# Hybrid decoder step on one Trainium2 core: hops of the stream merges moved within a step, up-projections ahead of turned probabilities, and two cache halves in other attention steps

## The chip, the cores and the metric

The kernel runs on one core of a Trainium2 chip. A core has four engines that compute, each with an instruction stream of its own, worked off in order: TensorE (PE, matrix products into PSUM), VectorE (DVE), ScalarE (ACT) and GpSimd (POOL). DMA queues move data between HBM and on-chip memory (SBUF); here SyncE, ScalarE and GpSimd issue them. The metric is the device time of one execution in microseconds (us), lower is better.

## The reference

One step of a two-layer decoder trunk serves a prompt of 1024 new tokens and 8 decode sequences of one token each. Layer 0 mixes with an mLSTM, layer 1 with multi-head latent attention; each is followed by a dense SwiGLU block. The change touches only the attention of layer 1, where both groups attend:

```python
def mla_attend_prompt(q_lat, q_rope, c_kv, k_r):   # per block of queries
    s = einsum('bqhc,bkc->bhqk', ql, c_kv) + einsum('bqhr,bkr->bhqk', qr, k_r)
    p = softmax(where(causal, s * MLA_SCALE, -inf))
    return einsum('bhqk,bkc->bqhc', p, c_kv)

def mla_attend_sample(q_lat, q_rope, c_new, kr_new, cache_latent, cache_k_rope, page_table, layer_idx):
    # per decode sequence: 8192 cached rows, read through a page table, and one new row
    c_all = concatenate([cache_latent[layer_idx, pages].reshape(past, 256), cn])
    kr_all = concatenate([cache_k_rope[layer_idx, pages].reshape(past, 64), krn])
    p = softmax((einsum('qhc,kc->hqk', ql, c_all) + einsum('qhr,kr->hqk', qr, kr_all)) * MLA_SCALE)
    return einsum('hqk,kc->qhc', p, c_all)
```

The outputs are the hidden states of both groups, the mLSTM states and the new latent and rotary rows.

## The kernel before

**Prompt attention** is cut into 32 blocks, one for each head and each group of 256 queries; a block of group G (0 to 3) attends to 2G + 2 tiles of 128 keys. A block's work is: two *scores* (`scores(0)` and `scores(1)`, one for each 128 queries, L1768 to L1775, with the row maximum on VectorE, L1776, and the exponential on ScalarE, L1785), *scale* (reciprocal on VectorE, L1793, and a pass over the probabilities on ScalarE, L1795), *turn* (128x128 transposes of the probabilities on TensorE, L1811, in groups of up to four, each emptied from PSUM into a high and a low part: ScalarE copies, L359 and L360, and GpSimd subtracts, L361; for the group on the diagonal ScalarE, L348, and VectorE, `wl`, L349), and *values* (L1833, three products for each key tile) with a copy out on ScalarE (L1836). Scores have four PSUM banks (`sc`), turns and values two (`mm`), the decode part two (`ss`). The keys and values of each head are *up-projected* from the latent rows (`make_k`, `make_v`, L365 to L367), emptied the same way.

A loop of 29 *steps* (`slot` 1 to 29 in the code) works on two blocks at a time: step s turns block s and does its values, and does scores and scale of block s + 1. Even heads take their groups in the order 0, 1, 2, 3, odd heads in the order 3, 2, 1, 0, so steps 3, 4, 11, 12, 19, 20 and 27 have the longest blocks and steps 7, 8, 15, 16, 23 and 24 the shortest. Steps 4, 12, 20 (group 3) and 2, 10, 18, 26 (group 2) hold a `make_k`; 5 to 7, 13 to 15, 21 to 23, and 8, 16 and 24 a `make_v`; steps 1, 3, 9, 11, 17, 19, 25 and 27 to 29 hold none.

**Decode attention** runs beside it as 32 *halves* (`Half`), each of 2048 cached rows: two halves make a unit, and two units make one decode sequence. For a half, GpSimd gathers the latent rows (`nat`, 2 MB in two indirect DMAs, four buffers) and the rotary rows (`nrp`, 0.5 MB, two buffers); VectorE transposes them in five pieces (`turn` in class `Sample`, tiles `tt`, L134, four buffers); TensorE multiplies them with the queries (`scores` in `Sample`, L143, 48 and 32 products). The code speaks of `first`, `second`, `third` and `fourth` of a half: `first` multiplies pieces 1, 4 and 0 and turns pieces 2 and 3 and piece 4 of the next half, `second` turns piece 0 of the next half and multiplies pieces 3 and 2, `third` turns piece 1 of the next half, `fourth` begins the softmax of the unit (`soft`) if the half is the second of a unit. In the step after that the probabilities are transposed and copied into place (`probs`, `pz`, L158, twelve copies on ScalarE and four on VectorE), and the *sums* (L173, 64 products) multiply them with both `nat` tiles of the unit, which frees these for the gathers of the halves four and five further on.

After the second unit of a sequence a *meeting* (`meet`) merges the parts of the 16 key streams: ten *hops* f0 to f9, alternately on VectorE ("V") and TensorE ("P"), in the order V P V P V V P V P V. The TensorE hops are L231, L239, L249 and L257. `hop(e)` issues the next one if it is for engine e, so a step's calls of `hop` say where each stands. Before, a step has the calls: V in `first`, P at the start of `second`, V at the end of `third`, P right before values, V in `fourth`; a meeting takes two steps.

TensorE's order is the order of the code. The other engines' orders are set by a scheduler from its own estimates, so they are to be read from the built program. SyncE only issues loads here.

## Time and profile before

| | us |
|---|---|
| median of 3 runs (2778.24 to 2785.95) | 2785.31 |
| profiled execution, its own time | 2779.62 |
| its span in the profile | 2777.1 |
| mean granted TensorE clock | 0.968 |
| step 1 of the loop starts about | 1424 |
| step 29 ends about | 1903 |

The attention loop is 479 of the 2777 us. Steps are told apart by the copy that ends each one's values (L1836): step 4 runs from about 1490 to 1506, step 5 to 1522, step 7 from 1533 to 1546, step 8 to 1559, step 12 from 1617 to 1640, step 19 from 1731 to 1752, step 21 from 1770 to 1783, step 22 to 1795, step 23 to 1809, step 26 from 1847 to 1870.

A row of a time line gives start, duration, engine, line, operation, what is written and read, and in brackets the idle time of the engine before it and what ended it. A row of a list of waits gives who waited for whom, the total, how many times, and the longest.

### The profile page before, as it was taken

What the parts mean: (1) busy time and instruction counts of PE and PEld (TensorE: products, weight loads), DVE (VectorE), ACT (ScalarE), POOL (GpSimd) and SP (SyncE); (2) the same over time, 40 slices, a digit from 0 to 9 for tenths busy, and PEclk for the clock granted to TensorE, in tenths of its full rate; (3) what the DMA queues carried; (4) which work ended last, traced back from release to release, by engine and by line L of the source; (5) the groups of instructions that cost most, each with busy time, mean ns of one, the idle gap of its engine ahead of it and who ended that gap; (6) DMA issues with size and microseconds to landing.
All of it is one profiled execution on the core that took longest, in us unless ns stands there. A gap on an engine that the chain in (4) does not pass through costs nothing.

```text
span 2777.1 us, 51994 instructions
## 1 busy us (share of the span) xinstructions
PE 2584.3 (93%) x20719; PEld 2442.9 (88%) x20719; DVE 1476.9 (53%) x3141; ACT 1194.5 (43%) x2715; POOL 868.4 (31%) x831
## 2 busy tenths in 40 slices
PE   8999989889999999999868887979988999999998
PEld 8998877889999999998757676767888999999997
DVE  4346678853344343455456667666574443434455
ACT  4212334434444444444246465645344444444442
POOL 1001002243333333323234454432323333333342
PEclk9999989999999999999879999989999999999999
DMA  5133556336655655453575657573533656555552
GB/s 183 38 76 95 129 144 155 106 86 129 119 115 116 123 116 117 86 188 119 160 266 179 220 196 261 200 256 97 192 100 86 125 117 124 116 116 117 117 140 100
DMA packets 350424, 383.67 MB, mean 138 GB/s; under 512 B 24441, under 2 KB 303358, under 8 KB 341862
## 3 DMA queue, kind: packets, MB, share of 16 engines
q0 software_dynamic: 38736, 174.68, 26.5%
q1 hardware_dynamic: 284502, 189.12, 23.2%
q10 hardware_dynamic: 26944, 16.56, 2.5%
q8 instruction: 162, 2.65, 0.4%
q14 instruction: 80, 0.66, 0.1%
HBM read 254.58 MB, written 125.70 MB: 137 GB/s over the span
## 4 chain that ended last, share of the span: by engine, by line
PE 66%; DVE 11%; DMA 11%; issue 5%; ACT 4%; POOL 3%; SPq 0%; ACTq 0%; POOLq 0%; DVEq 0%
PE sc L365 9%; PE sc L367 9%; PE sc L366 9%; PE ss L365 5%; PE ss L366 5%; PE mm L365 5%; PE ss L367 5%; PE mm L366 5%; PE mm L367 5%; DMA Gb<-G_d 2%; DMA nat<-in_cache_latent_dram,idx 2%; PE ss L143 2%; DVE wl L349 1%; PE mm L1833 1%; DVE tt L134 1%
## 5 line engine op out<-in xcount | busy, mean ns | idle before, releaser
L365 PE MATMUL ss<-ah,dh 128*128 128x344 f32 x864 | 277.5, 321 | 7.1 <-ACT st L1309 6.6
L1309 ACT COPY st<-ss 128x344 f32<-128x344 f32 x432 | 189.9, 441 | 215.4 <-PE ss L367 183.4
L366 PE MATMUL ss<-al,dh 128*128 128x344 f32 x864 | 277.6, 321 | 1.9 <-POOL al L349 1.9
L367 PE MATMUL ss<-ah,dl 128*128 128x344 f32 x864 | 276.9, 320 | 0.0
L348 ACT ACTIVATE wh<-wr 128x512 fp32r<-128x512 f32 (+2 forms) x161 | 130.6, 812 | 236.2 <-PE mm L366 127.2
L1311 POOL DMA_DIRECT2D x_d<-st x144 | 124.8, 867 | 244.1 <-ACT st L1309 240.2
L134 DVE STREAM_TRANSPOSE tt<-nat 128x1024 f32<-128x1024 f32 x128 | 156.8, 1232 | 52.3 <-PE ss L143 29.3
L365 PEld LDWEIGHTS ss<-ah,dh 128*128 128x128 f32 x864 | 163.0, 189 | 8.3 <-ACT st L1309 7.3
L366 PEld LDWEIGHTS ss<-al,dh 128*128 128x128 f32 x864 | 163.4, 189 | 2.3 <-POOL al L349 2.3
L349 POOL TENSOR_TENSOR al<-u,ah 128x512 fp32r<-128x512 f32 (+1 forms) x84 | 118.4, 1410 | 148.2 <-ACT ah L348 148.1
L367 PEld LDWEIGHTS ss<-ah,dl 128*128 128x128 f32 x864 | 163.1, 189 | 0.0
L349 DVE TENSOR_TENSOR wl<-S,wl 128x512 fp32r<-128x512 f32 x89 | 77.8, 874 | 156.9 <-ACT wl L348 125.8
L349 DVE TENSOR_TENSOR wl<-wr,wh 128x1024 fp32r<-128x1024 f32 (+2 forms) x92 | 106.0, 1153 | 51.2 <-ACT wh L348 43.4
L349 DVE TENSOR_TENSOR wh<-S,wh 128x512 fp32r<-128x512 f32 x91 | 68.6, 754 | 119.1 <-ACT wh L348 91.3
L1275 DVE TENSOR_TENSOR u<-u,sc 128x260 f32<-128x260 f32 (+1 forms) x168 | 70.8, 421 | 114.2 <-PE sc L367 113.0
L143 PE MATMUL ss<-tt,qbd 128*32 128x128 f32 x2560 | 98.4, 292 | 28.4 <-DVE tt L134 17.8
L1241 POOL TENSOR_TENSOR S<-S,wr 128x512 f32<-128x512 f32 x45 | 62.9, 1397 | 175.4 <-DVE wh L349 87.9
L1234 POOL TENSOR_TENSOR S<-wr 128x512 f32<-128x512 f32 x45 | 61.5, 1367 | 164.5 <-DMA wr<-in_ffn_w_gate_up_dram 162.0
L143 PEld LDWEIGHTS ss<-tt,qbd 128*32 128x32 f32 x2560 | 74.7, 117 | 41.6 <-issue 24.9
L365 PE MATMUL mm<-zh,wh 128*128 128x344 f32 x320 | 104.7, 327 | 7.0 <-DVE ot L693 6.9
L349 DVE TENSOR_TENSOR dl<-dr,dh 128x256 fp32r<-128x256 f32 x144 | 69.1, 480 | 73.0 <-ACT dh L348 73.0
L366 PE MATMUL mm<-zl,wh 128*128 128x344 f32 x320 | 103.8, 324 | 0.0
(928 smaller groups left out, 9226.7 us busy)
## 6 DMA issues: line engine op xcount, KB each, us to landing
x_d<-st POOLq DMA_DIRECT2D x144, 516.0 KB
wr<-in_ffn_w_gate_up_dram SPq DMA_DIRECT2D x98, 512.0 KB
dr<-in_ffn_w_down_dram SPq DMA_DIRECT2D x144, 128.0 KB
wr<-in_mlstm_w_in_dram SPq DMA_DIRECT2D x24, 512.0 KB
wr<-in_mlstm_w_out_dram SPq DMA_DIRECT2D x16, 512.0 KB
q<-qn_d SPq DMA_DIRECT2D x32, 256.0 KB
wr<-in_mla_w_o_dram SPq DMA_DIRECT2D x15, 512.0 KB
qn_d<-qx SPq DMA_DIRECT2D x16, 344.0 KB
```

The costliest lines, as they stand in the source:

```text
L134: self.V.transpose(out=tt, in_=src.rearrange("p s (c i) -> p c s i", i=32))
L143: self.nc.tensor.matmul(ps[32 * j:32 * j + 32], self.k.qbd[:, u // 4, cb], tt[:, c, 4 * j:4 * j + 4].rearrange("p s k -> p (s k)"), start= ...
L348: ins = nc.scalar.activation(hi, src, AF.Copy)
L349: self.low = e.tensor_tensor(lo, src, hi.bitcast(F32), op=ALU.subtract)
L365: mm(ps, wh, xh, start=start, stop=False, **kw)
L366: mm(ps, wh, xl, start=False, stop=False, **kw)
L367: self.last = mm(ps, wl, xh, start=False, stop=stop, **kw)
L1234: G(s, a21, a22, op=ALU.add)
L1241: G(s, s, a11, op=ALU.subtract)
L1275: V.tensor_tensor(u[:, 1], u[:, 1], ps, op=ALU.add)
L1309: nc.scalar.copy(st[:, cs], ps)
L1311: nc.gpsimd.dma_start(self.x_d[:, d], st, accum_op=ALU.add)
```

## The change

It has four parts, all in the loop over steps and in the decode part that runs beside it.

1. **Which steps take two halves.** Before, steps 8, 15 and 24 take two and all others one. After, steps 4, 11, 12, 19, 20 and 27 take two, steps 8, 16 and 24 none (the decode object itself then stands in for the half and issues only hops, the delayed gather and the end of a softmax), and all others one. There are 32 halves in both.
2. **Hops.** The V that stood at the end of `third` stands at the end of `second`, and the P that stood ahead of values stands behind them.
3. **Turns.** All groups of turned probabilities follow the up-projection; before, the first two groups stood ahead of it.
4. **Order in a step.** With one half, `third` comes behind values. With two, sums are possible after each of the two `second`, the first half's second scores come behind its sums, and `probs` is called for each half.

```diff
-DBL, LATE = (8, 15, 24), 30
+NONE, DBL, LATE = (8, 16, 24), (4, 11, 12, 19, 20, 27), 30
...
+    def fetch(self):
+        if self.due:
+            self.gather(self.due)
+            self.due = None
...
+    def first(self):
+        self.fetch()
+        self.late()
+        self.hop("V")
+
+    def second(self):
+        self.hop("P")
+        self.hop("V")
+
+    def third(self):
+        pass
+
+    def fourth(self):
+        self.hop("V")
...
         s.scores(u, (1, 4, 0))
-        if s.due:
-            s.gather(s.due)
-            s.due = None
+        s.fetch()
...
         s.hop("P")
         s.turn(u + 1, 0)
         s.scores(u, (3, 2))
+        s.hop("V")
 
     def third(self):
         self.s.turn(self.u + 1, 1)
-        self.s.hop("V")
...
-            halves = [sam.take() for _ in range(2 if slot in DBL else 1)]
-            u = halves[0]
+            halves = [sam.take() for _ in range(0 if slot in NONE else 2 if slot in DBL else 1)]
+            u = halves[0] if halves else sam
             far = Block(slot + 2)
             far.load()
             u.first()
-            groups = list(range(0, blk.nk, 2))
-            for j in groups[:2]:
-                blk.turn(j)
...
-            for j in groups[2:]:
+            for j in range(0, blk.nk, 2):
                 blk.turn(j)
             nxt.scores(0)
-            sam.probs()
-            u.second()
-            nxt.scale(0)
             if len(halves) > 1:
+                sam.probs()
+                u.second()
+                nxt.scale(0)
+                sam.sums()
                 u.third()
+                nxt.scores(1)
                 sam.hop("P")
                 u.fourth()
                 u = halves[1]
-                nxt.scores(1)
                 u.first()
+                sam.probs()
                 nxt.scale(1)
                 blk.values()
                 u.second()
+                sam.sums()
+            else:
                 sam.probs()
-                sam.sums()
-                u.third()
-                sam.hop("P")
-            else:
+                u.second()
+                nxt.scale(0)
                 nxt.scores(1)
                 sam.sums()
-                u.third()
                 nxt.scale(1)
-                sam.hop("P")
                 blk.values()
+            u.third()
+            sam.hop("P")
             u.fourth()
```

The lines of the changed file stand 19 to 21 further down: L239 is L260 there, L349 is L368, L365 to L367 are L384 to L386, L1776 is L1795, L1811 is L1830 and L1833 is L1852.

What the built programs show, at three places. First TensorE at the end of step 22 and the start of step 23, before: the last rows of values, the 48 products of the half's scores (L143), the turns of step 23 (`mm<-ct,wr`) and its up-projection (`sc<-swh,ckh` and so on).

```order
L1833 MATMUL mm_19739<-wl_19653,vt_17995 128x256
L1833 MATMUL mm_19739<-wh_19652,vt_17995 128x256
L143 MATMUL ss_19771<-tt_19735,qbd_15149 32x128 x8
L143 MATMUL ss_19771<-tt_19649,qbd_15149 32x128 x8
L143 MATMUL ss_19771<-tt_19702,qbd_15149 32x128 x8
L1811 MATMUL mm_19815<-ct_66,wr_19700 128x128
L1811 MATMUL mm_19815<-ct_66,wr_19733 128x128 x2
L365 MATMUL sc_19824<-swh_19262,ckh_13605 128x256
L366 MATMUL sc_19824<-swl_19264,ckh_13605 128x256
L367 MATMUL sc_19824<-swh_19262,ckl_13606 128x256
```

The same engine and place after the change:

```order
L1852 MATMUL mm_19866<-wl_19745,vt_18084 128x256
L1852 MATMUL mm_19866<-wh_19744,vt_18084 128x256
L260 MATMUL ss_19368<-ones_69,sS_19812 128x1
L143 MATMUL ss_19684<-tt_19882,qbd_15149 32x128 x8
L143 MATMUL ss_19684<-tt_19715,qbd_15149 32x128 x8
L143 MATMUL ss_19684<-tt_19793,qbd_15149 32x128 x8
L384 MATMUL sc_19930<-swh_19242,ckh_13605 128x256
L385 MATMUL sc_19930<-swl_19244,ckh_13605 128x256
L386 MATMUL sc_19930<-swh_19242,ckl_13606 128x256
```

The up-projection now follows the half's scores at once, and the turns stand behind its twelve matmuls. The meeting's hop L260 (L239 before) stands behind values. Where it stood before shows the second place, TensorE in step 23 before the change, from the end of the second scores to values:

```order
L1775 MATMUL sc_19893<-mk_14404 128x128
L173 MATMUL ss_19403<-nat_19135,pz_14408 32x256 x16
L173 MATMUL ss_19403<-nat_19208,pz_14408 32x256 x16
L239 MATMUL ss_19403<-ones_69,sS_19942 128x1
L1833 MATMUL mm_19947<-wh_19813,vt_17817 128x256
L1833 MATMUL mm_19947<-wh_19813,vt_17817 128x128
```

Sums, hop, values: the hop was ahead of values there, and it is behind them in the rows above.

The third place is VectorE in a step whose next half has only just been gathered. Before, that is step 22; `nat_19582` is the fresh tile, `wl` the last split of the turned probabilities that this step's values need, `mx` the maximum of the scores.

```order
L134 STREAM_TRANSPOSE tt_19649<-nrp_19611 128x1024
L349 TENSOR_TENSOR wl_19653<-mm_19663,wh_19652 128x256
L134 STREAM_TRANSPOSE tt_19702<-nat_19582 128x1024
L349 TENSOR_TENSOR wl_19653<-mm_19663,wh_19652 128x128
L1776 TENSOR_REDUCE mx_19689<-sc_19691 128x1
L1782 TENSOR_SCALAR mx_19689<-mx_19689,rqt_14290 128x1
L134 STREAM_TRANSPOSE tt_19735<-nat_19582 128x1024
```

After the change the fresh tile is `nat_19502`, in step 21, behind the double step 20:

```order
L134 STREAM_TRANSPOSE tt_19609<-nat_19502 128x1024
L1795 TENSOR_REDUCE mx_19596<-sc_19598 128x1
L134 STREAM_TRANSPOSE tt_19666<-nat_19502 128x1024
L1801 TENSOR_SCALAR mx_19596<-mx_19596,rqt_14290 128x1
L219 TENSOR_REDUCE rm_19668<-ss_19368 128x1
L1795 TENSOR_REDUCE mx_19629<-sc_19631 128x1
L1812 RECIPROCAL sm_19597<-sm_19597 128x1
L221 SCALAR_TENSOR_TENSOR nb_19670<-rm_19668,nb_19357 128x1
L1801 TENSOR_SCALAR mx_19629<-mx_19629,rqt_14290 128x1
L134 STREAM_TRANSPOSE tt_19711<-nat_19502 128x1024
L368 TENSOR_TENSOR wl_19587<-mm_19588,wh_19586 128x256
```

The split `wl` has moved from beside the first turn of the fresh tile to behind three turns of it and both maxima.

## The prediction

> **What bounds the kernel now.** I read the page first, then the stretches around the attention steps, then who waits for whom inside them.

> ```profile
> PE 2584.3 (93%) x20719; PEld 2442.9 (88%) x20719; DVE 1476.9 (53%) x3141; ACT 1194.5 (43%) x2715; POOL 868.4 (31%) x831
> PE 66%; DVE 11%; DMA 11%; issue 5%; ACT 4%; POOL 3%; SPq 0%; ACTq 0%; POOLq 0%; DVEq 0%
> ```

> TensorE is the bound over the whole span. The next view gives busy times, granted clock, DMA share and GB/s of stretches; the first row is nearly all of the steps that the change touches (2 to 29), the others are steps 19, 26 and 4.

> ```profile
> core 0: us, PE busy (x) PEld busy (x) DVE busy (x) ACT busy (x) POOL busy (x), PEclk, DMA share, GB/s
> 1452.00:1903.00 451.00, 385.47 (x4837) 314.53 (x4838) 301.96 (x638) 250.80 (x680) 199.95 (x194) 0.94 0.60 209
> 1731.00:1752.00 21.00, 15.65 (x157) 12.16 (x158) 11.27 (x28) 13.74 (x36) 9.46 (x9) 0.92 0.40 128
> 1847.00:1870.00 23.00, 18.92 (x174) 14.77 (x170) 11.79 (x28) 13.98 (x36) 10.80 (x10) 0.87 0.58 201
> 1490.00:1506.00 16.00, 15.59 (x202) 13.30 (x190) 11.80 (x26) 10.29 (x27) 8.95 (x8) 1.00 0.80 304
> ```

> In the steps TensorE idles 451.0 - 385.5 = 65.5 us, and its clock is 0.94. The change adds no work and takes none away, so it can only win these 65.5 us, plus at most 0.06 x 451 = 27 us of clock. Who ended TensorE's waits there (total, times, longest):

> ```profile
> PE mm L1811 <- ACT wr L1795: 15.6, 8, 3.6
> PE ss L239 <- DVE sS L236: 13.8, 7, 4.1
> PE ss L143 <- DVE tt L134: 5.5, 2, 2.8
> PE mm L1811 <- ACT spl L360: 4.5, 7, 1.1
> PE ss L257 <- DVE w L253: 4.1, 3, 1.8
> PE ss L231 <- DVE sm L1793: 3.8, 2, 2.7
> PE ss L173 <- ACT pz L158: 3.6, 3, 1.8
> PE ss L257 <- DVE nb L200: 2.9, 1, 2.9
> PE ss L143 <- DVE sm L1793: 2.8, 1, 2.8
> PE ss L143 <- DVE olat L260: 1.3, 1, 1.3
> ```

> **What goes.** *Meetings*: L231, L239, L257 and L260 are hops of one, so they cost 13.8 + 4.1 + 3.8 + 2.9 + 1.3 = 25.9 us. One, in step 19:

> ```profile
> 1743.41 3.66 PE L173 MATMUL ss<-nat,pz 128*32 128x256 f32 x64
> 1749.09 0.38 PE L239 MATMUL ss<-ones,sS 1*128 1x1 f32 x2 [2.02 <-DVE sS L236]
> 1749.40 0.45 PE L1833 MATMUL mm<-wh,vt 128*128 128x256 f32 x2
> 1752.41 1.52 PE L143 MATMUL ss<-tt,qbd 128*32 128x128 f32 x48
> ```

> The hop L239 stands ahead of values (L1833, 24 matmuls, 1749.40 to 1752.41, 3.0 us), which do not need it. After the change VectorE's half comes before those matmuls and TensorE's behind them. I take all 25.9 as gone; what is late next is the product with the scores of the next half.

> *Probabilities*: the waits for scaled probabilities (L1795) sum to 15.6 us. Two of the eight stand in steps 3 and 19, where no up-projection runs:

> ```profile
> 1472.35 0.90 PE L1811 MATMUL mm<-ct,wr 128*128 128x128 f32 x3 [3.63 <-ACT wr L1795]
> 1733.47 0.98 PE L1811 MATMUL mm<-ct,wr 128*128 128x128 f32 x7 [2.75 <-ACT wr L1795]
> ```

> The other six, 9.2 us, get an up-projection of 2 to 3 us as cover: 9.2 gone.

> *Doubles in light steps*: the waits for `tt` (5.5), for `pz` (3.6) and L143 for `sm` (2.8) lie in and around steps 8, 15 and 24: 11.9 us gone. Together **47.0 us** go.

> **What comes.** First, where a gathered tile arrives, seen twice:

> ```profile
> 1540.75 3.66 PE L173 MATMUL ss<-nat,pz 128*32 128x256 f32 x64
> 1545.22 1.93 PE L143 MATMUL ss<-tt,qbd 128*32 128x128 f32 x48
> 1552.80 0.22 PE L1775 MATMUL sc<-mk 128*128 128x128 f32 x1
> 1553.25 1.25 DVE L134 STREAM_TRANSPOSE tt<-nat 128x1024 f32<-128x1024 f32 x1 [1.62 <-DMA nat<-in_cache_latent_dram,idx]
> 1555.80 1.52 PE L143 MATMUL ss<-tt,qbd 128*32 128x128 f32 x48 [2.78 <-DVE sm L1793]
> ...
> 1777.48 3.71 PE L173 MATMUL ss<-nat,pz 128*32 128x256 f32 x64
> 1788.96 1.25 DVE L134 STREAM_TRANSPOSE tt<-nat 128x1024 f32<-128x1024 f32 x1 [0.55 <-DMA nat<-in_cache_latent_dram,idx]
> 1790.13 0.25 DVE L349 TENSOR_TENSOR wl<-mm,wh 128x128 fp32r<-128x128 f32 x1
> 1790.31 0.27 DVE L1776 TENSOR_REDUCE mx<-sc 128x1 f32<-128x128 f32 x1
> ```

> The sums (L173) free a tile, GpSimd gathers the next half into it, and VectorE can turn that one 1553.25 - 1544.41 = 8.8 us or 1788.96 - 1781.19 = 7.8 us after the sums end: 8.3 us. TensorE needs 1545.22 to 1553.02 = 7.8 us for a light step up to the end of its second scores (48 + 32 score products of the half, up-projection, turns, both scores). VectorE works in order, so whatever stands behind that first turn waits with it. In the rows at 1790.13 only one small split and the maxima stood behind it, and TensorE arrived just then. The changed order puts more there:
> - Steps 5 and 21, behind a double that ends in sums: two more turns, two maxima and small ones stand ahead of the last split `wl`, which values need. By durations that is 3 turns at 1.25, two maxima of about 0.6, splits of 0.4 and 0.25, and 1.1 of small ones = 6.7 us, so `wl` comes at 8.3 + 6.7 = 15.0; TensorE arrives at about 7.8 + 1.6 (two more groups of turns) = 9.4. A hole of 5.5 each, 11.0.
> - Steps 7 and 23: first turn, maximum, second turn, `wl` = 3.3, at 11.6; TensorE has values (12 matmuls, 1.5) and a light step with smaller scores (6.3): 7.8. Holes of 4.0, 8.0. Step 14 likewise 2.5.
> - Steps 11, 12 and 27: the double's first half does sums, its second half wants the new tile turned twice for the next step: 8.3 + 2.5 = 10.8. TensorE has second scores (2.4, 2.1 and 0.8), score products 1.5, values 3.0 and 1.0 more: 7.9, 7.6 and 6.3. Holes of 2.9, 3.2 and 4.5, sum 10.6.

> That is 32.1 us. If gathers come at 7.8 and half of VectorE's work slips in elsewhere it is 16; at 8.8, with eight holes, 36.

> Second, steps 4, 19 and 20 end a softmax in their first half and want its probabilities (`pz`) in the second. The three doubles of before waited 3.6 us for `pz`; the twelve copies on ScalarE take 0.25 us each, 3.0:

> ```profile
> 1619.89 0.99 ACT L158 COPY pz<-pT 32x64 f32<-32x64 f32 x4
> 1620.79 0.58 ACT L359 ACTIVATE wh<-mm 128x512 fp32r<-128x512 f32 x1
> 1621.28 0.56 ACT L360 COPY spl<-mm 128x512 f32<-128x512 f32 x1
> ```

> So between 3.6 and 7.5; I take 6.0, since in step 19 the copy of values is put ahead of the twelve.

> Third, turns behind an up-projection. A group of turned probabilities or an up-projected tile costs ScalarE 0.58 + 0.56 = 1.14 us, and two banks hold the groups. Before, the up-projection's matmuls ran while the first two groups were emptied; now its own tiles are emptied first, and the third group finds both banks full. Upper bound: 1.14 plus what is left of the other copy, some 1.5 us in steps 2, 10, 13, 18 and 26 and 2.0 in 4, 12 and 20 (four groups): 13.5. Lower bound: L1811's waits for `spl` above, 4.5 us in 7, 0.64 each, times 8 = 5.1. I take 9.0.

> New waits: 32.1 + 6.0 + 9.0 = **47.1 us**. Transfers are the same in number and size; those that move cost nothing beyond the holes counted. The net is 47.1 - 47.0 = +0.1 us, on the profiled execution's 2779.62: **2780 us**. That execution lies 0.2% under the median of the runs, 2785.31; I count from it. Under about 0.3% (8 us) a measurement of this kernel cannot tell a change from none.

> **The clock, weighed.** Step 19 had holes of 2.75 and 2.02 us (rows above) and was granted 0.92; step 26, with 4.1 us idle, the longest wait of L239, 0.87; step 4, idle for 0.4 us, kept 1.00: 0.08 x 21 = 1.7 us and 0.13 x 23 = 3.0 us lost. So a hole costs 2 to 3 us of clock at either size; some ten go and some ten come, and I count zero. [...]

> **Rivals.**
> - *The stalls stay on VectorE.* If TensorE reaches values later than I reckon, or if the gathers land some 2 us sooner because the light steps no longer hold two halves, steps 5, 7, 14, 21 and 23 hide theirs (21.5 of the 32.1). For it: DMA is busy 0.60 in the steps, and at 1790.13 the same pattern cost nothing. Against it: the 2.78 us at 1555.80. Time: 2780 - 21.5 = 2758.
> - *Longer holes cost more clock* (the other side). If holes of 4 to 5.5 us cost the 3.0 us of step 26, and those of up to 2 us nothing, the seven of 2.9 us and more at 5, 7, 12, 21, 23, 27 and 11 cost 21, against 7 to 9 given back for the three or four long ones of before. It decides from holes of about 3 us on. Time: 2780 + 13 = 2793. [...]
> - *The meetings are not spread.* VectorE's order is not the code's: in step 23 the vector for the last product stands behind two turns of a fresh tile. If the hops keep half of their waits: 2780 + 13 = 2793.

> **How the numbers follow.** Forecast, no measurable change: 0.37, its own range 2772 to 2788. Stalls hidden: 0.35, all faster. Clock: 0.21, and meetings not spread: 0.07, both slower. So faster 0.35, within 0.3% 0.37, slower 0.28. Low end: new waits at 16 + 3.6 + 5.1 = 24.7 instead of 47.1, 22 less, and a little clock: 2755. High end: 36 + 7.5 + 13.5 = 57, 10 more, and two thirds of the clock's 13: 2799. What is left out on both sides is under 2 in 10.

> **What would show it.** Right: no waits of L239's and L257's successors on VectorE beyond 1 us; six fewer waits for L1795; waits of values for `wl` in steps 5 and 21 of about 5 us, and of score products for `tt` at the ends of 11, 12 and 27 of about 3 to 4. Wrong: values in 5, 7, 21 and 23 start without a wait, or TensorE's idle time in the steps falls under 45 us (faster) or the clock there falls under 0.92 (slower).

## The result, and the profile after

The changed kernel takes 2816.76 us (median of 4 runs, 2815.52 to 2818.12), the kernel before beside it 2785.43 us (4 runs, 2778.24 to 2785.95): ratio 1.0119, 95% interval 1.0101 to 1.0136. It is slower by 1.2%, outside the range of the prediction. The page of the profile after, busy times and the chain of work that ended last:

```profile
PE 2607.6 (93%) x20719; PEld 2465.0 (88%) x20719; DVE 1479.9 (53%) x3141; ACT 1194.6 (42%) x2715; POOL 868.5 (31%) x831
PE 69%; DVE 11%; DMA 8%; ACT 5%; issue 4%; POOL 2%; SPq 0%; another core or an unknown queue 0%; ACTq 0%; POOLq 0%; DVEq 0%
```

The instructions are the same in number, yet TensorE is busy for 23 us more. The windows view of the steps shown before, now 1452 to 1938 (the columns as in the prediction):

```profile
1452.00:1938.00 486.00, 400.49 (x4840) 326.80 (x4830) 302.99 (x631) 251.11 (x677) 199.12 (x194) 0.91 0.55 195
```

The same work takes 486.0 us where it took 451.0: **20.0 us more idle** (85.5 where there were 65.5) and **15.0 us more busy** (400.5 where there were 385.5). The second goes with the clock, 0.91 where there was 0.94: 0.09 x 486 is 44 us lost to it, 0.06 x 451 was 27. The split hangs a little on where the stretch begins: from the last value product of step 1 to that of step 29 the time goes from 455.4 to 490.3 us, 17.2 of it idle and 17.7 busy. Who ended TensorE's waits there (total, times, longest):

```profile
PE mm L1830 <- ACT spl L379: 27.4, 16, 4.7
PE mm L1830 <- ACT wr L1814: 16.0, 7, 3.6
PE ss L143 <- issue: 9.0, 20, 1.0
PE ss L173 <- ACT pz L158: 7.6, 6, 1.9
PE mm L1852 <- ACT spl L379: 6.3, 2, 3.6
PE mm L1852 <- ACT wh L367: 4.1, 3, 1.8
PE ss L143 <- DVE olat L281: 4.0, 3, 2.1
PE mm L1852 <- DVE wl L368: 2.6, 3, 0.9
PE ss L143 <- DVE tt L134: 2.5, 1, 2.5
PE ss L278 <- DVE w L274: 1.7, 1, 1.7
```

The change moved the line numbers by 19 to 21: L1830 is the turns' line (L1811 before), L379 ScalarE's copy into `spl` (L360), L380 GpSimd's subtraction (L361), L1814 the scaling (L1795), L1852 values (L1833), L281 the last copy of a meeting (L260). The first row matters most: turns waited for `spl` for 4.5 us before, and for 27.4 us now. The waits of hops have all but gone. The waits for scaled probabilities (L1814) should have lost 9 us of 15.6, and are 16.0.

What such a wait is made of shows at the head of step 10, in the time line of GpSimd, ScalarE and TensorE after:

```profile
1594.65 1.00 POOL L117 DMA_INDIRECT nrp<-in_cache_k_rope_dram,idx  x1 [4.29 <-DVE tt L134]
1595.96 0.96 POOL L117 DMA_INDIRECT nrp<-in_cache_k_rope_dram,idx  x1 [0.30 <-issue]
1596.93 2.50 POOL L380 TENSOR_TENSOR kt<-spl,kt 128x512 fp32r<-128x512 f32 x2
1599.38 2.52 POOL L380 TENSOR_TENSOR wl<-spl,wh 128x512 fp32r<-128x512 f32 x2
...
1593.71 0.58 ACT L379 COPY spl<-sc 128x512 f32<-128x512 f32 x1
1594.17 0.61 ACT L378 ACTIVATE kt<-sc 128x512 fp32r<-128x512 f32 x1
1594.66 0.60 ACT L379 COPY spl<-sc 128x512 f32<-128x512 f32 x1
1595.13 0.63 ACT L378 ACTIVATE wh<-mm 128x512 fp32r<-128x512 f32 x1
1598.24 0.59 ACT L379 COPY spl<-mm 128x512 f32<-128x512 f32 x1 [2.49 <-POOL kt L380]
...
1598.88 0.55 PE L1830 MATMUL mm<-ct,wr 128*128 128x128 f32 x3 [4.44 <-ACT spl L379]
```

and at the same place before:

```profile
1587.71 0.96 POOL L117 DMA_INDIRECT nrp<-in_cache_k_rope_dram,idx  x1 [1.53 <-DVE pz L158]
1588.68 1.31 POOL L361 TENSOR_TENSOR wl<-spl,wh 128x512 fp32r<-128x512 f32 x1
1592.37 2.54 POOL L361 TENSOR_TENSOR kt<-spl,kt 128x512 fp32r<-128x512 f32 x2
...
1590.03 0.58 ACT L360 COPY spl<-sc 128x512 f32<-128x512 f32 x1 [0.54 <-POOL wl L361]
1592.47 0.58 ACT L360 COPY spl<-sc 128x512 f32<-128x512 f32 x1 [0.71 <-POOL wl L361]
...
1589.14 0.49 PE L1811 MATMUL mm<-ct,wr 128*128 128x128 f32 x3
```

After, the two up-projected tiles (`kt`) fill both `spl` buffers by 1595.26. A buffer comes free only when GpSimd has subtracted, 1.25 us a tile, and GpSimd's queue first holds two gathers of rotary rows, the first of which had itself waited 4.29 us for VectorE. So the copy of the first turned group starts at 1598.24 instead of about 1595.6, and TensorE's third group, which needs that bank, waits 4.44 us. Before, turned groups went first in the same chain; it was the up-projected tiles that waited (0.54 and 0.71 us), and they are not needed until the next head.

Half of the 27.4 us stands in three such waits: 4.7 us in step 2, 4.4 in step 10 and 4.5 in step 26. In steps 2 and 26 the rows are the same: two gathers of rotary rows, the first of which waited 6.76 and 8.03 us for VectorE, stand on GpSimd ahead of the two `kt`. In step 18, where the two gathers came before the `kt` were copied, the wait is 2.0 us.

### The profile page after: what moved, and what is told of

Same layout as the page of the kernel before. It is cut to its first block, busy times and chain, and to the rows that moved or that the text cites. A ratio compares the mean times of both kernels' runs of the same rounds, so it can differ in the third digit from the quotient of the medians.

```text
span 2815.4 us, 51982 instructions
## 1 busy us (share of the span) xinstructions
PE 2607.6 (93%) x20719; PEld 2465.0 (88%) x20719; DVE 1479.9 (53%) x3141; ACT 1194.6 (42%) x2715; POOL 868.5 (31%) x831
## 4 chain that ended last, share of the span: by engine, by line
PE 69%; DVE 11%; DMA 8%; ACT 5%; issue 4%; POOL 2%; SPq 0%; another core or an unknown queue 0%; ACTq 0%; POOLq 0%; DVEq 0%
PE sc L384 10%; PE sc L386 10%; PE sc L385 10%; PE mm L384 5%; PE ss L384 5%; PE ss L385 5%; PE ss L386 5%; PE mm L385 5%; PE mm L386 5%; PE ss L143 2%; PE ss L173 2%; DMA Gb<-G_d 2%; DVE tt L134 2%; DVE wl L368 1%; PE mm L1852 1%
## 5 line engine op out<-in xcount | busy, mean ns | idle before, releaser
L384 PE MATMUL ss<-ah,dh 128*128 128x344 f32 x864 | 277.4, 321 | 6.7 <-ACT st L1328 6.3
L386 PE MATMUL ss<-ah,dl 128*128 128x344 f32 x864 | 276.8, 320 | 0.0
L367 ACT ACTIVATE wh<-wr 128x512 fp32r<-128x512 f32 (+2 forms) x161 | 130.6, 813 | 237.4 <-PE mm L385 130.5
L134 DVE STREAM_TRANSPOSE tt<-nat 128x1024 f32<-128x1024 f32 x128 | 156.9, 1232 | 50.6 <-PE ss L143 18.5
L384 PEld LDWEIGHTS ss<-ah,dh 128*128 128x128 f32 x864 | 162.9, 189 | 7.6 <-ACT st L1328 6.7
L368 POOL TENSOR_TENSOR al<-u,ah 128x512 fp32r<-128x512 f32 (+1 forms) x84 | 118.4, 1410 | 148.0 <-ACT ah L367 147.9
L386 PEld LDWEIGHTS ss<-ah,dl 128*128 128x128 f32 x864 | 162.9, 189 | 0.0
L368 DVE TENSOR_TENSOR wl<-S,wl 128x512 fp32r<-128x512 f32 x89 | 78.6, 883 | 156.7 <-ACT wl L367 125.7
L368 DVE TENSOR_TENSOR wl<-wr,wh 128x1024 fp32r<-128x1024 f32 (+2 forms) x92 | 105.3, 1146 | 53.6 <-ACT wh L367 46.3
L368 DVE TENSOR_TENSOR wh<-S,wh 128x512 fp32r<-128x512 f32 x91 | 68.2, 749 | 119.7 <-ACT wh L367 92.1
L143 PE MATMUL ss<-tt,qbd 128*32 128x128 f32 x2560 | 98.7, 286 | 26.9 <-DVE tt L134 12.4
L384 PE MATMUL mm<-zh,wh 128*128 128x344 f32 x320 | 104.9, 328 | 6.4 <-DVE ot L712 6.4
L143 PEld LDWEIGHTS ss<-tt,qbd 128*32 128x32 f32 x2560 | 72.9, 114 | 41.6 <-issue 29.1
L368 DVE TENSOR_TENSOR dl<-dr,dh 128x256 fp32r<-128x256 f32 x144 | 69.4, 482 | 72.1 <-ACT dh L367 72.1
```

The source lines that it names most:

```text
L134: self.V.transpose(out=tt, in_=src.rearrange("p s (c i) -> p c s i", i=32))
L143: self.nc.tensor.matmul(ps[32 * j:32 * j + 32], self.k.qbd[:, u // 4, cb], tt[:, c, 4 * j:4 * j + 4].rearrange("p s k -> p (s k)"), start= ...
L367: ins = nc.scalar.activation(hi, src, AF.Copy)
L368: self.low = e.tensor_tensor(lo, src, hi.bitcast(F32), op=ALU.subtract)
L384: mm(ps, wh, xh, start=start, stop=False, **kw)
L386: self.last = mm(ps, wl, xh, start=False, stop=stop, **kw)
```

## Experiments

Theory A: most of the loss is the turns behind the up-projection, through this chain. Theory B: it is the moved doubles. All ratios are to the kernel before, run beside it on the same chip, as the result of each run gives them; ratios of plain medians differ from them by up to 0.0012. 0.1% is 2.8 us. Where an expectation gives a time, it is to be read against the 2785 us of the kernel before above, since that kernel ran at 2771 to 2783 us on the chips used here. The new order in a double step (the fourth part of the change) goes with it in every kernel made from the change.

| kernel | turns behind | doubles moved | hops spread | ratio (95% interval) |
|---|---|---|---|---|
| e2_turns_behind_only | yes | | | 1.0085 (1.0058 to 1.0112) |
| e6_doubles_only | | yes | | 1.0072 (1.0045 to 1.0100) |
| e3_meetings_only | | | yes | 0.9975 (0.9962 to 0.9989) |
| e4_doubles_back | yes | | yes | 1.0055 (1.0038 to 1.0072) |
| e1_turns_ahead | | yes | yes | 1.0106 (1.0081 to 1.0131) |
| e7_hops_back | yes | yes | | 1.0111 (1.0085 to 1.0138) |
| the change | yes | yes | yes | 1.0119 (1.0101 to 1.0136) |

### The parts one by one

e1, the change with these lines back ahead of the up-projection, and e2, the kernel before without them (there all groups are turned behind):

```diff
+            groups = list(range(0, blk.nk, 2))
+            for j in groups[:2]:
+                blk.turn(j)
...
-            for j in range(0, blk.nk, 2):
+            for j in groups[2:]:
                 blk.turn(j)
```

> The changed kernel, with the first two groups of turned probabilities ahead of the up-projection again. Theory A (the turns cost it: behind the up-projection each group's copy waits in a chain of two spl buffers and GpSimd's subtractions): the waits for spl, 33.7 us in the profile after, fall back to about 5, the waits for scaled probabilities stay at some 16 to 20, and with some of the clock back the time is 2772 to 2788. Theory B (the doubles beside the long blocks cost it): the spl waits go but others take their place, 2803 to 2815.

> The kernel before, with only the turns put behind the up-projection. Theory A: the waits for spl rise from 4.5 us to about 30, and the time by 20 to 35 us, to 2805 to 2820. Theory B: the cover for the scaled probabilities (9 us) and the new spl waits about cancel, 2778 to 2792.

e3, the kernel before with the V of `third` at the end of `second`, and `third` and the P behind values; e4, the change with the old doubles:

```diff
-NONE, DBL, LATE = (8, 16, 24), (4, 11, 12, 19, 20, 27), 30
+NONE, DBL, LATE = (), (8, 15, 24), 30
```

> The kernel before, with only the hops of a meeting spread (and the turn of the third part put behind values). If each of the 25.9 us of waits for hops was worth its length: about 2760. If the next wait takes their place (the score products of the next half wait for the turned tile that now comes later): 2775 to 2786.

> The changed kernel, with one half in every step and doubles in 8, 15 and 24 again (turns behind the up-projection, hops spread). Theory A: the spl waits stay near 30 us, and the time is 2800 to 2815. Theory B: 2765 to 2785.

e6, the change without the other two parts, and e7, the change with the hops back:

> The kernel before with only the doubles moved (none in 8, 16, 24, two in 4, 11, 12, 19, 20, 27, with the double step's new body). Theory A (the doubles cost by themselves: the long steps lose the sums that covered the scaled probabilities, and ScalarE's twelve copies stand ahead of the scaling): 2800 to 2815, with waits of turns for scaled probabilities near 29 us where there were 15.6. Theory B (they cost only together with the spread hops): 2776 to 2790.

> The changed kernel with the hops of a meeting at their old places (turns behind the up-projection, doubles moved). If the spread hops are still worth about 20 us there: 2825 to 2840. If they are worth as little as alone (6 us): 2812 to 2824. If they cost something beside the moved doubles: under 2810.

Measured: the turns alone cost 0.85%, as A said; the moved doubles alone cost 0.72%, which B said of e1 and A, revised, of e6. Both are true, and expectations that set one against the other failed where they left the other out: by A, e1 was to be near the kernel before, and by B, e4. The hops gain 0.25% alone and nothing that can be told beside the other two (1.0111 to 1.0119).

Added up the three give +1.32%, near the +1.19% of the change, but that is luck, since the pairs do not add: turns and doubles cost 1.11% (e7) where their sum is 1.57%, and doubles and hops 1.06% (e1) where it is 0.47% (single figures are good to some 0.1 to 0.3%, and the kernels ran on two chips). Putting the turns back ahead in the change won nothing that can be told (1.0119 to 1.0106). One reason shows in the waits: beside the moved doubles the turns behind the up-projection also cover what the doubles uncover, 32.2 us of waits for scaled probabilities in e6 and 16.0 in the change. Why doubles and hops together cost more than apart was not tried.

TensorE's waits, first in e2 (steps 2 to 29), then in e3:

```profile
PE mm L1811 <- ACT spl L360: 28.3, 17, 4.7
PE mm L1811 <- ACT wr L1795: 8.5, 3, 3.6
```

```profile
PE ss L143 <- DVE olat L260: 11.9, 6, 4.3
PE ss L231 <- DVE sm L1793: 5.4, 2, 2.7
PE ss L257 <- DVE w L253: 2.8, 1, 2.8
```

In e2 the up-projection does cover scaled probabilities: 15.6 us became 8.5. The chain takes back three times that. In e3 the waits of hops fell from 24.6 us to 8.2, but the next score products wait 11.9 us (1.3 before) for the last copy of a meeting, since TensorE's last hop now stands with nothing behind it but these products.

In e6 the scaled probabilities are the cost, 32.2 us where there were 15.6. First the waits, then the head of step 11 in the time line of e6 (TensorE, then ScalarE), then the same stretch of the kernel before:

```profile
PE mm L1829 <- ACT wr L1813: 32.2, 12, 4.2
PE ss L173 <- ACT pz L158: 8.6, 7, 3.0
PE mm L1851 <- ACT wh L366: 7.3, 2, 6.4
```

```profile
1599.95 0.98 PE L1829 MATMUL mm<-ct,wr 128*128 128x128 f32 x7 [3.62 <-ACT wr L1813]
...
1597.21 1.51 ACT L158 COPY pz<-pT 32x64 f32<-32x64 f32 x6 [0.27 <-issue]
1598.75 1.15 ACT L1813 ACTIVATE wr<-wr,sm 128x1024 f32<-128x1024 f32 x1
```

```profile
1595.23 3.66 PE L173 MATMUL ss<-nat,pz 128*32 128x256 f32 x64
1603.63 1.22 PE L1811 MATMUL mm<-ct,wr 128*128 128x128 f32 x8
```

In the kernel before, step 10 ran sums (L173, 3.66 us) between its second scores and values; they held TensorE while ScalarE went on to the second scaling (1602.66 to 1603.81 in its time line), and step 11 turned the probabilities without a wait for it. With the doubles moved, step 10 has no sums, and the turns wait 3.62 us, ScalarE having copied `pz` for some 2 us just ahead of the scaling. How much of the wait is the missing sums and how much these copies, no run tells apart. In e6 the ten waits over 1 us from step 3 on stand in steps 3, 8, 10, 11, 15, 17, 18, 24, 26 and 27, each behind a step without sums; before, the six over 1 us, in 3, 5, 12, 19, 21 and 23, likewise. (The reverse does not hold: before, steps 7, 10, 14, 17, 26 and 28 also stand behind a step without sums, and none of them waits for 1 us.) With the doubles moved, sums fall on other steps; 10, 17 and 26, each ahead of a longer block, lose theirs, and steps 11, 18 and 27, which had no wait over 1 us, wait 3.5 to 3.9 us each.

### The chain

e5 and e9 are e2 with another way to the remainder of an up-projected tile; e13 and e10 put the edit of e5 into the kernel before and into the change, e14 into e6, e15 into e7. At each call that makes such a tile:

```diff
-                    make_k(h + 1, split_p, "sc")
+                    make_k(h + 1, split_d, "sc")
```

`split_d` lets VectorE subtract straight from PSUM: neither `spl` nor GpSimd nor ScalarE's second copy is used. e9 keeps that copy (`split_2`):

```diff
+        def split_2(hi, lo, ps, shape):
+            nc.scalar.activation(hi, ps, AF.Copy)
+            nc.scalar.activation(lo, ps, AF.Copy)
+            V.tensor_tensor(lo, ps, hi.bitcast(F32), op=ALU.subtract)
```

> The kernel before with the turns behind the up-projection (as in e2_turns_behind_only), and the remainder of the up-projected tiles taken on VectorE straight from PSUM, without a spl buffer and without GpSimd. Theory A (the third group waits because the two spl buffers and GpSimd's queue are held by the up-projection's own subtractions): the waits of turns for spl fall from 28.3 us to under 8, and the time from 2802 to between 2775 and 2788. Rival (ScalarE's copies alone set it; here it copies 0.56 us less per up-projected tile): the waits stay at 14 or more, 2790 to 2800. Second rival (VectorE, with some 0.6 us more per tile, is late for something else): spl waits go and waits for wl or wh come, 2790 to 2805.

> As e5_upproj_on_vector, but ScalarE copies each up-projected tile twice again (the second copy goes into the low tile and is overwritten by VectorE's subtraction, so it only keeps ScalarE's 0.56 us). This tells the two causes left by e5 apart: e5 took away both ScalarE's second copy and GpSimd's subtraction with its spl buffers, its time was that of the kernel before, but 16.9 us of waits for spl stayed. If GpSimd and the spl buffers made the cost: still near the kernel before (ratio under 1.003), waits for spl under 20 us. If ScalarE's copies made it: near e2_turns_behind_only (ratio 1.006 to 1.009), waits for spl near 28 us.

> The kernel before, with only the remainder of the up-projected tiles on VectorE. If GpSimd's chain cost the kernel before next to nothing (its waits of turns for spl are 4.5 us): ratio 0.997 to 1.002, and the 0.8% that the same edit gave the turns behind the up-projection was the chain's cost there. If VectorE gives as much here: 0.990 to 0.995, and the turns behind the up-projection cost as much as ever.

> The whole changed kernel, with only the remainder of the up-projected tiles taken on VectorE from PSUM. If the spl chain costs in it what it cost alone (23 us): ratio to the kernel before 1.001 to 1.005, what is left being the moved doubles. If the doubles' own waits come in its place (alone they cost 0.7%): 1.006 to 1.010. If VectorE, which does more beside the doubles, becomes late: over 1.010.

> e6_doubles_only with the remainder of the up-projected tiles on VectorE. If the moved doubles cost through waits for scaled probabilities that the turns meet uncovered (32.2 us in e6, against 15.6 before): ratio 1.004 to 1.008, and those waits stay over 25 us. If they cost through GpSimd's chain: 1.002 or less.

> e10_change_upproj_on_vector with the hops at their old places. If the spread hops are worth 0.25% there as alone: ratio 1.000 to 1.003. If nothing beside the moved doubles: 0.997 to 0.9995.

| kernel | GpSimd (above) | VectorE |
|---|---|---|
| before | 1 | e13: 0.9982 (0.9965 to 0.9998) |
| turns behind | 1.0085 | e5: 1.0007 (0.9993 to 1.0021); e9: 1.0033 (1.0018 to 1.0048) |
| doubles moved | 1.0072 | e14: 1.0063 (1.0043 to 1.0084) |
| turns and doubles | 1.0111 | e15: 1.0037 (1.0021 to 1.0053) |
| the change | 1.0119 | e10: 0.9983 (0.9972 to 0.9995) |

The edit gives the kernel before 0.18%, the turns 0.78% and the whole change 1.36%: with GpSimd out of the way of the up-projected tiles the change is **0.17% faster** than before (0.08% by plain medians), though no faster than the kernel before with the same edit (0.9982): what it gains and what it costs then cancel, which the prediction had forecast with the chain in place. No expectation of e10 had it so fast, and e15 came out slower than both of its. By e9 some two thirds of the 0.78% (0.52) lie with GpSimd and its buffers and a third (0.26, at the limit of what can be told between two chips) with ScalarE's second copy; e9 lies between its two expectations and meets neither. So the cost goes when the up-projected tiles leave GpSimd and its buffers, which shows A's mechanism in time, and the rival that ScalarE's copies alone set it falls. In the waits for `spl` A is shown only in part, first in e5 and then in e9:

```profile
PE mm L1811 <- ACT spl L360: 16.9, 19, 2.4
```

```profile
PE mm L1817 <- ACT spl L360: 23.2, 19, 2.9
```

In e5 under 8 us was expected. The turned groups still pass ScalarE, `spl` and GpSimd among themselves; what went is the longest waits, 4.7 to 2.4 us. The doubles are different: e14 still costs 0.63%, and its turns wait for scaled probabilities nearly as long as in e6, so theirs is the lost cover (with the copies of `pz`) and not the chain:

```profile
PE mm L1829 <- ACT wr L1813: 28.7, 12, 3.6
```

The hops gain 0.54% beside turns and doubles once the chain is gone (e15 to e10, on two chips). Why they gained nothing with the chain in place was not tried.

### Hops, and what might beat both

e8 is the kernel before with one line moved:

```diff
         s.scores(u, (3, 2))
+        s.hop("V")
 
     def third(self):
         self.s.turn(self.u + 1, 1)
-        self.s.hop("V")
```

> The kernel before with one line moved: VectorE's half of a hop from the third part to the end of the second, while TensorE's half stays ahead of values. In e3_meetings_only the waits of hops fell from 24.6 to 8.2 us, but the next score products waited 11.9 us (1.3 before) for the last copy (olat) of a meeting, since TensorE's half stood behind values with nothing after it. If that is the cause, both waits are short here, and the time is 2755 to 2770. Rival (the last hop is late for another reason, VectorE's queue): 2770 to 2782.

0.9969 (0.9954 to 0.9984), 0.3% faster than before, where 0.5 to 1.1% was expected; this is the range of the rival. Waits of hops fell from 24.6 to 7.6 us, and those for the last copy are half of e3's (6.1 us in two waits for 11.9 in six); whether VectorE's queue makes that copy late, as the rival has it, the list of waits does not tell. Others grew:

```profile
PE ss L143 <- DVE tt L134: 7.4, 2, 4.4
PE ss L173 <- ACT pz L158: 6.8, 4, 3.4
PE ss L143 <- DVE olat L260: 6.1, 2, 3.6
```

Against 5.5, 3.6 and 1.3 before: of 17 us saved, 10 are met again. The rest of the runs are built on e8. e11 turns behind the up-projection only behind a step without sums, and uses VectorE there (`sums` now returns True where it runs):

```diff
+            ahead = 2 if summed else 0
+            split_u = split_p if summed else split_d
-            for j in groups[:2]:
+            for j in groups[:ahead]:
...
-                sam.sums()
+                summed = sam.sums()
```

> e8_hop_v_early, with the turns behind the up-projection only in those steps whose predecessor ran no sums, and with the up-projected tile's remainder on VectorE in those steps. In the traces so far turns waited 1.5 us or more for scaled probabilities only in steps behind one without sums; six such steps of the kernel before have an up-projection. If that is the rule: waits for scaled probabilities fall from 16.0 to about 7 us and the ratio to the kernel before from 0.9969 to 0.992 to 0.995. Rival (what VectorE takes over makes it late elsewhere): 0.996 to 1.000.

e12 is e8 with e5's edits, e16 is e11 with the first late group's remainder on VectorE too, e17 is e8 with all up-projected tiles on VectorE, and e18 is e17 with e11's rule for the turns:

> e8_hop_v_early and e5_upproj_on_vector together: all turns behind the up-projection, its remainder on VectorE, VectorE's half of a hop early. If the two add: ratio 0.995 to 0.999 (0.9969 and 1.0007 multiplied: 0.9976). If the waits left for spl in e5 (16.9 us) hide the waits of hops: over 0.999.

> e11_turns_behind_where_needed, with the remainder of the first group of turns behind an up-projection on VectorE too, so that the third group does not find both spl buffers in use. If the 16.8 us of waits for spl left in e11 come from that: they fall under 11 us and the ratio from 0.9953 to 0.991 to 0.994. If ScalarE's copies alone are left in them, or VectorE is late for it: 0.995 to 0.998.

> e8_hop_v_early with the remainder of every up-projected tile on VectorE, and all turns at their old places. If the two add: 0.9969 x 0.9982 = 0.9951, that is 0.9935 to 0.9965, as fast as e11, and moving turns gains nothing. If VectorE's added work eats what its early half of a hop gains: 0.997 to 0.999, and e11's turns were worth some 0.3%.

> e17_hop_early_vector with the turns behind the up-projection in the steps whose predecessor ran no sums. If the cover for the scaled probabilities is real once GpSimd is out of the chain: waits for scaled probabilities fall by some 7 us and the ratio lies 0.002 to 0.003 under that of e17. If ScalarE's copies alone take it back: within 0.001 of e17.

Measured: e11 0.9953 (0.9938 to 0.9968), e12 0.9999 (0.9985 to 1.0012), e16 1.0007 (0.9991 to 1.0024), e17 0.9978 (0.9963 to 0.9993), e18 0.9998 (0.9981 to 1.0014). e11 is the fastest that was run, 10 us under the kernel before (just between its two expectations), but e18, which differs from it only in the tiles of the steps whose turns stay ahead, is at no difference on another chip, and e11's interval overlaps that of e8. The clean pair is e17 and e18, on one chip: they differ in the turns alone. Waits of turns in e17, then in e18:

```profile
PE mm L1811 <- ACT wr L1795: 14.9, 8, 3.8
PE mm L1811 <- ACT spl L360: 4.3, 7, 1.2
```

```profile
PE mm L1812 <- ACT spl L361: 19.0, 13, 3.4
PE mm L1812 <- ACT wr L1796: 9.2, 4, 3.8
```

The cover is real, 14.9 us become 9.2, and it does not pay even with VectorE: those for `spl` rise by 14.7, and the time does not fall (it rises by 0.2%, with intervals that overlap), which neither expectation of e18 had. In e12 the two gains did not add, and in e16 the waits for `spl` fell to 11.3 us, but turns wait 10.6 us for VectorE instead, and it is slower than both of its expectations.

## Why the prediction was wrong, by its own steps

- **"Turns behind an up-projection ... I take 9.0": the step that failed most.** Waits of turns for `spl` rose from 4.5 to 27.4 us; alone the part cost 0.85%, some 24 us, where cost and cover were to cancel. The sum reckoned with ScalarE's 1.14 us for each group and with two `mm` banks. It left out that every tile holds one of two `spl` buffers until GpSimd has subtracted, 1.25 to 1.3 us, and that GpSimd's queue also holds gathers that wait for VectorE. In steps 4 and 20, where the gather stands behind the two `kt`, the wait was 1.8 us where 2.0 was the upper bound; in 2, 10 and 26 it was 4.4 to 4.7 where 1.5 was. The rows of GpSimd in step 10 stood in the profile before.
- **"The clock ... I count zero": failed.** TensorE was busy 15.0 us longer for the same work. Holes did not come one for one: in steps 2 to 29 the records show 11 spells at half clock before (57 us) and 19 after (92 us).
- **"The other six, 9.2 us, get an up-projection ... as cover": right alone, undone by another part.** The turns alone saved 7.1 (one of the six, 0.2 us in step 17, has no up-projection). That moved doubles also move the sums, the older cover, away from steps 10, 17 and 26 was missed: it doubled these waits in e6, and in the change they are 16.0 where 6.4 were expected.
- **"I take all 25.9 as gone": right in the waits, wrong in the time.** In the change hops wait 3.4 us and the products behind a meeting 4.0. Alone the part gains 7 us, since score products wait in their stead; beside the moved doubles alone it seems to cost (e6 to e1, on two chips), and beside both other parts nothing can be told until the chain is gone.
- **"Where a gathered tile arrives ... 32.1": half.** In 5, 7, 14, 21 and 23 values wait 13.0 us (rows of L1852 above) for 21.5, and of the ends of 11, 12 and 27 only that of 11 waits, 2.5 us, for 10.6 in all. The place was right, and in e6 step 21 has its hole in full, 6.4 us. In step 5 of the change `wl` came 15.4 us after the sums, near the 15.0 of the prediction, but TensorE came to values only 12.5 us after them and not 9.4, so the hole was 3.6 us. The last link there was ScalarE's copy into `spl`, put behind exponentials that had waited for VectorE's maxima, and not `wl` itself.
- **"I take 6.0" for `pz`**: 7.6, about right. Of the waits in light steps (11.9), those for `tt` and L143 for `sm` went; the 2.5 us for `tt` that are left are the ones at the end of step 11.

As to the rivals: "the stalls stay on VectorE" came half true and was outweighed; "the meetings are not spread" is false; "longer holes cost more clock" had the sign, with too small a price (13 us for the 15.0 above), and the loss did not go by the length of a hole alone: in the change the 4.44 us of step 10 went with one window at half clock, the 3.63 us in step 11 with two (below). Of the signs named beforehand, the clock in the steps fell under 0.92, which was to mean slower; of the signs of being right, the waits for scaled probabilities went only from eight to seven, and a hop still waits 1.7 us. That the turns' chain would be a rival of its own was not seen at all.

By sizes: the forecast had 0.1 us more idle and no clock; the steps show 20.0 and 15.0. Against the forecast, the idle time has 13.9 us more for turns that wait for `spl` (27.4 for 4.5 + 9.0), 9.6 more for scaled probabilities, 7.4 more for hops and the products behind them, 3.6 more that the profile puts down to no one and 1.6 more for `pz`; the gathered tiles cost 16.6 less. That the miss in idle time is not larger is luck: without the last term it would have been some 36 us.

## What to carry to other kernels

Where two kinds of work pass the same chain of small buffers (here ScalarE, two `spl` buffers, GpSimd), their order is a priority: put ahead what is needed first, and size a move by the slowest link of the chain and by what else stands in that engine's queue, not by the engine that waits. Before moving work out of a step, ask whose wait it was hiding: where the sums stood they covered ScalarE's scaling, and with the doubles moved turns waited 17 us more for it. And parts of a change are tested one at a time, in pairs, since they need not add, and then without the suspected chain: here a change that lost 1.2% lost nothing with one helper replaced.

## What the runs showed of the hardware

```profile
core 0: us, PE busy (x) PEld busy (x) DVE busy (x) ACT busy (x) POOL busy (x), PEclk, DMA share, GB/s
1592.77:1596.18 3.41, 1.67 (x12) 1.25 (x10) 2.74 (x3) 2.98 (x6) 1.22 (x2) 1.00 0.37 114
1596.18:1599.59 3.41, 0.70 (x5) 0.67 (x6) 0.00 (x0) 1.21 (x3) 3.40 (x4) 1.00 0.57 158
1599.59:1603.01 3.42, 3.42 (x15) 2.80 (x17) 1.31 (x3) 1.03 (x3) 2.31 (x2) 0.50 0.02 5
```

A window with 1.67 us of TensorE's work (49%) was followed by full clock, one with 0.70 us (21%) by half. With both whole traces cut so, behind a window at full clock in which TensorE was busy under 40%, the next was at half clock in 17 of 17 cases before and 20 of 20 after; at 40 to 50%, in 4 of 6 and 7 of 15; at 50% and more, in 5 of 734 and 10 of 719. So, as an estimate from these counts, a hole of about 2 us could cost a window, 1.7 us of work, or nothing, by where it fell; eight of the 19 spells at half clock in the steps after lasted two windows. What sets the clock no run shows beyond these counts.

The chips used here differed in a small way that matters at 0.3%: waits of L143 that the profile puts down to no one ("issue", 5.4 us before and 9.0 after) stand in the lists of waits of 11 kernels (before, after, e1 to e4, e13, e14 and e16 to e18; 1.6 to 9.0 us) and in none of those of e5, e6, e8, e9 and e10. These five ran on two chips, where the kernel before took 2771 and 2773 us instead of 2777 to 2785 on the others. What these waits are no run shows. A difference under some 0.3% between ratios from different chips is therefore no result here.
